# A hybrid gated-DeltaNet and retention layer: a pool of its own for the second merge's matrices, and the transposed v in the projections' PSUM banks with two buffers

## The chip, the cores and the metric

One Trainium2 chip, one of its cores. The metric is the device time of one execution in microseconds (us), the lower the better. TensorE (PE) multiplies matrices into PSUM, VectorE (DVE), ScalarE (ACT) and GpSimd (POOL) work element by element, SyncE (SP) issues most of the DMA transfers; ScalarE and POOL issue some of their own. Each engine takes its instructions strictly in order, so an instruction that waits holds up all that stand behind it on that engine.

## The reference

One layer of a latent transformer over 256 context tokens and 1024 latent tokens, 1024 wide. After an RMS norm with modulation, one input projection feeds two groups of four heads: a gated delta rule (GDN) in both directions and a retention in both directions. Both are normed, gated, projected out and added; a SwiGLU follows, and a last norm. What the change touches is the delta rule, in chunks (the kernel takes 128 tokens as a chunk):

```python
G = jnp.cumsum(gc, axis=-1)
decay = jnp.where(incl, jnp.exp(jnp.where(incl, diff, 0.0)), 0.0)   # diff = G_i - G_j
A = jnp.where(strict, jnp.einsum('nbhid,nbhjd->nbhij', kb, kc) * decay, 0.0)
sol = lax.linalg.triangular_solve(A + jnp.eye(CHUNK), rhs, left_side=True, lower=True, unit_diagonal=True)
qk = jnp.einsum('nbhid,nbhjd->nbhij', qc, kc) * decay
...
v_new = u_c - jnp.einsum('bhck,bhkv->bhcv', w_c, S)
o = jnp.einsum('bhck,bhkv->bhcv', q_c, S) + jnp.einsum('bhij,bhjv->bhiv', qk_c, v_new)
S = gl * S + jnp.einsum('bhck,bhcv->bhkv', k_c, v_new)
```

So for every chunk, head and direction a lower triangular matrix I + A has to be inverted before the scan over the chunks can use it. The norms of k go into the exponent (line 673), which is the "key factors in the exponent" of the kernel's name.

## The kernel before, in words

All matrix products are in float32; a product of full precision is made of three products of split operands (hi and lo parts), which is why the projections come in lines 371, 372, 373 and the convolution's in lines 611, 612, 613. Ten tiles of 128 tokens: 0 and 1 are context, 2 to 9 latent. The program is written in the order of the stages, and a scheduler then mixes the instructions of neighbouring stages on each engine, as far as data, buffers and PSUM banks allow. The order of the work is therefore set by what waits for what, by the order in which a buffer is handed out, and by the scheduler; the rows of it are shown with the change.

The stages in question, in the program's order:

- **Projections** (`token_major`, lines 389 to 399): 24 matrix products per tile and group g of 256 columns, in the PSUM banks "pa" (tile tm, three banks). g 0 and 1 are the retention's v, 2 and 3 its k, 4 and 5 its q, 6 and 7 its gate, 8 and 9 the gate z of the delta rule. They are TensorE's filler wherever another stage waits.
- **Convolution of k, q and v** (`conv_block`, lines 602 to 624): one head is one block of 1280 columns in three chunks in the banks "pc" (tile b), evacuated twice by ScalarE (u and y, lines 614 and 615), four taps on VectorE (line 621), a SiLU (line 624).
- **Preparation of a chunk** (`pre`, lines 700 to 737): products k k' (kk, line 705), transposed q and its norms (qt, lines 710 and 712), k q' (kq, line 715), all in the three banks "pb". For each direction the decays gw come by DMA (line 718), POOL masks them into e (line 722), ScalarE takes exponentials (lines 726 and 735), VectorE multiplies them onto kk and kq (ut and sp, lines 730 and 732), POOL makes the decayed q (line 736), and the results are stored to the scratch tensors un and sd. The pool "gp" holds these tiles, two buffers each.
- **Inversion** (`invert`, lines 743 to 771): the 32x32 diagonal blocks of a batch of chunks are inverted by forward substitution on VectorE: a copy (line 759), 62 operations one after the other (lines 765 and 767), a transposed copy (line 769), and a store to xd. The batches are `BATCH = [[0,1,2,9],[3,8,4,7],[5,6]]`.
- **Merge** (`merge`, lines 791 to 838, with the loads of `blocks`): the whole matrices U (2 MB, line 782) and the inverted blocks, once into U (line 786) and once into t64 (line 787, after a memset by POOL, line 784), then four rounds of small products (lines 806, 813 and 816, 829, 833) in the banks "pb", each with an evacuation by VectorE (xt, lines 809 and 830) or ScalarE (lines 819, 822, 835), and a store to sd (line 837). U and t64 have one buffer in the pool "gm", so the next batch's loads wait until the last one's matrices are stored.
- **The transposed v** (lines 849 to 859): after each head's convolution of v, ten transposes in three groups (vT, in "pb"), copied by ScalarE with a scale into vt (one buffer) and stored by ScalarE's queue.
- **The scan** (`step`, lines 893 to 948): ten steps, both directions side by side; step 0 begins with Tr (line 919) and needs its packed tile pk (line 898). The rest of the projections (g 2 to 5) lies between its first two steps and the others, then the retention.

The program's order is: gate projections, `solve(0)` and `solve(1)` (preparation and inversion of batches 0 and 1), v with its convolution and transposes, preparation of batch 2, `merge(0)`, `invert(2)`, `merge(1)`, `merge(2)`, the z projections, scan. A PSUM ring and a buffer ring hand out their places in this order, whatever the scheduler does.

Of the kernel before, what the change touches and what calls it, by code (L numbers as in the profile page):

```python
# [8 lines left out]
F32 = mybir.dt.float32  # L9
# [8 lines left out]
P = 128  # L18
# [7 lines left out]
H = 4  # L26
# [12 lines left out]
def build(nc, tc, ap, dbg=None, stop=None, marks=None):  # L39
# [3 lines left out]
    def pool(name, bufs=1, side=None, space=None):  # L43
        kw = {}
        if side is not None:
            kw["side"] = side
        if space is not None:
            kw["space"] = space
        if space is not DRAM:
            kw["reuse_waits"] = "tile"  # L50
        es = ExitStack()
        p = es.enter_context(tc.tile_pool(name=name, bufs=bufs, **kw))
        root.push(es)
        p_close[id(p)] = es
        return p
# [3 lines left out]
    def close(p):  # L59
        p_close.pop(id(p)).close()  # L60
# [5 lines left out]
    def checkpoint(name):  # L66
        if dbg is not None:
            marks.append((name, int(nc.cur_bb.bb.instructions[-1].name.split("-")[-1])))
        if stop == name:
            raise Stop()  # L70
# [19 lines left out]
    def bank_a(name):  # L90
        return bank("pa", name)

    def bank_b(name):
        return bank("pb", name)
# [96 lines left out]
    try:  # L191
# [387 lines left out]
        ps = bank_b("G")  # L579
# [14 lines left out]
        ps = bank_b("GT")  # L594
# [5 lines left out]
        CV = pool("cv", side="right")  # L600
# [87 lines left out]
        checkpoint("rg")  # L688
        close(R2)
        close(W2)  # L690
        GP = pool("gp")
        GU = pool("gu")
        GI = pool("gi")

        BATCH = [[0,1,2,9],[3,8,4,7],[5,6]]
        where = {t: (b, c) for b, ch in enumerate(BATCH) for c, t in enumerate(ch)}
# [3 lines left out]
        def pre(t):  # L700
            b, c = where[t]
            kc = load(GP, kd[t], "kc", 2)
            pk = bank_b("kk")
            for h in range(H):
                T.matmul(pk[:, h * P:(h + 1) * P], kc[:, h, :], kc[:, h, :], start=True, stop=True)
            if t >= 2:
                qc = load(GP, qd[t - 2], "qc", 2)
                pn = bank_b("qt")
# [7 lines left out]
            for d in range(2):  # L716
                gw = GP.tile([P, H, P], F32, tag="gw", name="gw", bufs=2)
                SY.dma_start(gw.rearrange("p h i -> p (h i)"),
                             grow_d[c8(t, d), :].rearrange("a b -> (a b)").partition_broadcast(P))
                e = GP.tile([P, H, P], F32, tag="e", name="e", bufs=2)  # L720
                sg = 1 if d == 0 else -1
# [5 lines left out]
                if t >= 2:  # L727
                    sp = GP.tile([P, 2, H, P], F32, tag="sp", name="sp", bufs=2)
                ut = GU.tile([P, H, P], F32, tag="ut", name="ut", bufs=2)
# [13 lines left out]
        def invert(b):  # L743
# [4 lines left out]
            xd = xds[b] = dr.tile([4 * nb, 1024], F32, tag="xd%d" % b, name="xd%d" % b)  # L748
            yr = GI.tile([P, 1024], F32, tag="yr", name="yr", bufs=1)
            for k in range(4):  # L750
                SY.dma_start(yr[k:2 * nb:4].rearrange("r (i j) -> r i j", j=32),
                             un[b][q32[k]].rearrange("i e u j -> (e u) i j")[:, :, q32[k]])
            L = GI.tile([P, 1024], F32, tag="L", name="L", bufs=3)
            X = GI.tile([P, 1024], F32, tag="X", name="X", bufs=2)
# [18 lines left out]
        def blocks(b):  # L773

            nu = len(BATCH[b]) * H
            nb = 4 * nu

            def blk(dram, k):
                return dram.rearrange("(u b) (i j) -> b i u j", b=4, j=32)[k]

            uu = GM.tile([P, 2, len(BATCH[b]), H, P], F32, tag="U", name="U%d" % b, bufs=1)
            SY.dma_start(uu.rearrange("p e c h j -> p e (c h) j"), un[b])
            tt = GM.tile([P, 2, nu, 64], F32, tag="t64", name="t64", bufs=1)
            G.memset(tt, 0.0)
            for k in range(4):
                SY.dma_start(uu[q32[k]].rearrange("p e c h j -> p (e c h) j")[:, :, q32[k]], blk(xds[b][:2 * nb], k))
                SY.dma_start(tt[q32[k]].rearrange("p e u j -> p (e u) j")[:, :, (k % 2) * 32:(k % 2) * 32 + 32],
                             blk(xds[b][2 * nb:], k))
            return uu, [uu[:, 1 - d] for d in range(2)], [tt[:, d] for d in range(2)]
# [59 lines left out]
        for h in range(H):  # L849
            y = newy()  # L850
            conv_block(8 + h, y, False)
            for t0, n in ((0, 2), (2, 4), (6, 4)):
                ps = bank_b("vT")
                for t in range(t0, t0 + n):
                    T.transpose(ps[:, (t - t0) * P:(t - t0 + 1) * P], y[:, t * P:(t + 1) * P], ident)
                vt = CV.tile([P, 4, P], F32, tag="vt", name="vt", bufs=1)
                for t in range(n):
                    S.activation(vt[:, t], ps[:, t * P:(t + 1) * P], AF.Copy, scale=sv3[:, t0 + t, h:h + 1])
                S.dma_start(vd[t0:t0 + n, :, h, :].rearrange("t p j -> p t j"), vt[:, :n])
# [1 line left out]
        checkpoint("v")  # L861
        RP = pool("rp", side="right")
        rope = RP.tile([P, TT, P], F32, tag="rope", name="rope")
        GM = pool("gm")
        for t in BATCH[2]:
            pre(t)
        checkpoint("pre2")
        merge(0)
        SY.dma_start(rope, ap["rope"])
# [7 lines left out]
            token_major(g, LAT, fin_gate, S, W)  # L877
        checkpoint("rgz")
        close(GM)
        close(GI)  # L880
        close(GU)
        close(GP)


        SC = pool("sc", bufs=2, side="right")
# [764 lines left out]
```

## Time and profile before

| | us |
|---|---|
| median of 3 runs | 1491.97 (1490.93 to 1492.1) |
| profiled execution | 1485.42 |
| its span, first to last instruction | 1483.3 |
| mean granted TensorE clock | 0.977 |
| TensorE busy | 1404.5 (95%) |
| first product kk / first U<-un / first merge product | 282.8 / 401.8 / 432.5 |
| last transposed v on TensorE / last vt copy | 395.5 / 411.3 |
| first step of the scan (Tr) behind the last merge | 540.0 |

Times are counted from the start of the span. An engine's busy time is the union of its instructions' spans; in the groups by line the columns are line, engine, operation, result and operands, count, then busy us and mean ns of one, then idle time in front of them and what ended it. "issue" as a releaser means that the profile shows nothing that was waited for. "SPq" rows are transfers as SyncE issues them.

### The profile page before, as it was taken

Reading aid. Unit: us, or ns where it says so; the run is one execution under the profiler, and the core shown is the slowest. Engines: PE = TensorE matmul, PEld = TensorE weight load, DVE = VectorE, ACT = ScalarE, POOL = GpSimd, SP = SyncE. Lnnn points to the kernel's source line nnn. Section 1 sums busy time; section 2 is a strip of 40 time slices with the busy share of each in tenths; the row PEclk is TensorE's granted clock in tenths of the full one; section 3 lists DMA queues with packets and bytes.
Section 4 is the critical chain, followed back from the end, with each engine's and each line's share of the span. In section 5 each row is a group of like instructions: output and inputs, shape, how many; then the busy total and the mean of one; then the engine's idle time right before and its main releaser. Section 6 shows DMA issues by size and latency. Waiting matters only on the chain.

```text
span 1483.3 us, 24109 instructions
## 1 busy us (share of the span) xinstructions
PE 1404.5 (95%) x8919; PEld 1205.9 (81%) x8919; DVE 974.3 (66%) x1856; ACT 616.4 (42%) x1328; POOL 591.8 (40%) x501
## 2 busy tenths in 40 slices
PE   7999999987979899999799899999999999999997
PEld 2898888976978899899588688877888888788886
DVE  6566789279848345788777876656555555657586
ACT  5543564477451121245444533323333332454444
POOL 0120011133114343234135588999555553334321
PEclk9999999998989899999899999999999999999999
DMA  8536686587687645996633265765222242786863
GB/s 321 210 104 205 188 249 198 181 267 224 202 245 204 236 160 209 415 378 221 218 115 114 86 208 214 265 242 178 107 107 106 106 148 79 240 278 199 297 199 114
DMA packets 176565, 298.14 MB, mean 201 GB/s; under 512 B 43496, under 2 KB 93880, under 8 KB 172096
## 3 DMA queue, kind: packets, MB, share of 16 engines
q1 hardware_dynamic: 124896, 253.17, 49.5%
q10 hardware_dynamic: 49072, 35.83, 7.9%
q0 software_dynamic: 2480, 7.60, 1.5%
q8 instruction: 70, 1.15, 0.3%
q14 instruction: 47, 0.39, 0.1%
HBM read 206.60 MB, written 89.96 MB: 200 GB/s over the span
## 4 chain that ended last, share of the span: by engine, by line
PE 39%; POOL 6%; DMA 2%; issue 1%; DVE 1%; ACT 1%; POOLq 0%; ACTq 0%; DVEq 0%
PE ffn L1341 7%; PE ffn L1339 6%; PE ffn L1340 6%; PE fo L1465 4%; PE fo L1467 4%; PE fo L1466 4%; PE op L1198 2%; PE op L1200 2%; PE op L1199 2%; DMA wd<-tw 2%; POOL ws L1312 1%; POOL tw L1393 1%; POOL tw L1392 1%; POOL tw L1395 1%; POOL tw L1394 1%
## 5 line engine op out<-in xcount | busy, mean ns | idle before, releaser
L371 PE MATMUL tm<-whi,hhi 128*128 128x256 f32 (+1 forms) x704 | 201.3, 289 | 4.5 <-ACT xa L384 1.8
L372 PE MATMUL tm<-wlo,hhi 128*128 128x256 f32 (+1 forms) x704 | 201.8, 288 | 2.7 <-DVE wlo L345 2.7
L373 PE MATMUL tm<-whi,hlo 128*128 128x256 f32 (+1 forms) x704 | 199.5, 287 | 0.0
L371 PEld LDWEIGHTS tm<-whi,hhi 128*128 128x128 f32 x704 | 134.2, 192 | 8.7 <-ACT xa L384 2.5
L372 PEld LDWEIGHTS tm<-wlo,hhi 128*128 128x128 f32 x704 | 135.1, 192 | 4.9 <-DVE wlo L345 3.3
L1339 PE MATMUL ffn<-t,whi 128*128 128x512 f32 x352 | 136.9, 390 | 1.4 <-ACT whi L344 1.4
L1341 PE MATMUL ffn<-t,wlo 128*128 128x512 f32 x352 | 137.0, 390 | 0.8 <-DVE wlo L345 0.8
L1340 PE MATMUL ffn<-t,whi 128*128 128x512 f32 x352 | 137.0, 389 | 0.0
L373 PEld LDWEIGHTS tm<-whi,hlo 128*128 128x128 f32 x704 | 134.4, 192 | 0.9 <-DVE hlo L314 0.2
L344 ACT ACTIVATE whi<-wraw 128x512 fp32r<-128x512 f32 (+2 forms) x98 | 75.1, 770 | 136.0 <-PE ffn L1340 81.9
L344 ACT ACTIVATE whi<-ws 128x512 fp32r<-128x512 f32 x88 | 55.6, 632 | 171.6 <-PE ffn L1340 123.9
L345 DVE TENSOR_TENSOR wlo<-ws,whi 128x512 fp32r<-128x512 f32 x88 | 96.0, 1092 | 45.4 <-ACT whi L344 45.2
L1465 PE MATMUL fo<-whi,ahi 128*128 128x512 f32 x308 | 119.3, 389 | 0.9 <-ACT ahi L344 0.9
L1466 PE MATMUL fo<-wlo,ahi 128*128 128x512 f32 x308 | 119.9, 389 | 0.0
L1467 PE MATMUL fo<-whi,alo 128*128 128x512 f32 x308 | 119.0, 390 | 0.0
L345 DVE TENSOR_TENSOR wlo<-wraw,whi 128x512 fp32r<-128x512 f32 (+2 forms) x92 | 98.6, 1073 | 17.7 <-ACT whi L344 17.6
L1339 PE MATMUL ffn<-b,whi 128*128 128x512 f32 x264 | 104.2, 395 | 4.1 <-ACT whi L344 4.1
L1341 PE MATMUL ffn<-b,wlo 128*128 128x512 f32 x264 | 103.9, 393 | 0.7 <-DVE wlo L345 0.7
L1340 PE MATMUL ffn<-b,whi 128*128 128x512 f32 x264 | 103.7, 393 | 0.0
L611 PE MATMUL b<-hhi,whi 128*128 128x512 f32 (+1 forms) x256 | 95.6, 373 | 2.1 <-ACT y L615 1.9
L613 PE MATMUL b<-hhi,wlo 128*128 128x512 f32 (+1 forms) x256 | 95.2, 372 | 0.0
L612 PE MATMUL b<-hlo,whi 128*128 128x512 f32 (+1 forms) x256 | 95.1, 372 | 0.0
(446 smaller groups left out, 3465.6 us busy)
## 6 DMA issues: line engine op xcount, KB each, us to landing
adaw<-ada_w SPq DMA_DIRECT2D x48, 512.0 KB, 4.9
pk<-sd SPq DMA_DIRECT2D x16, 1536.0 KB, 10.9
wraw<-wfi SPq DMA_DIRECT2D x44, 512.0 KB, 3.6
ar<-ad SPq DMA_DIRECT2D x33, 512.0 KB, 4.5
w<-wfo SPq DMA_DIRECT2D x22, 512.0 KB, 5.7
wd<-tw SPq DMA_DIRECT2D x11, 1024.0 KB, 4.8
ad<-act SPq DMA_DIRECT2D x20, 512.0 KB, 3.0
raw<-wd SPq DMA_DIRECT2D x20, 512.0 KB, 5.1
```

The lines of the kernel that those rows point to most:

```text
L344: S.activation(hi, raw, AF.Copy)
L345: e.tensor_tensor(lo, raw, hi.bitcast(F32), ALU.subtract)
L371: T.matmul(o, hhi[:, k, tsl], whi[:, k % 4, :], start=(k == 0), stop=False)
L372: T.matmul(o, hhi[:, k, tsl], wlo[:, k % 4, :], start=False, stop=False)
L373: T.matmul(o, hlo[:, k, tsl], whi[:, k % 4, :], start=False, stop=(k == KT - 1))
L611: T.matmul(o, whi[:, k, :], hh, start=(k == 0), stop=False)
L1339: T.matmul(o, whi[:, k, :], xhi(xn, slice(0, 4), k), start=(first and k == 0), stop=False, **kw)
L1340: T.matmul(o, whi[:, k, :], xlo(xn, slice(0, 4), k), start=False, stop=False, **kw)
L1341: T.matmul(o, wlo[:, k, :], xhi(xn, slice(0, 4), k), start=False, stop=(k == 3), **kw)
L1465: T.matmul(po[g][i], ahi[:, ts], whi, start=(j == 0 and not kw), stop=False, **kw)
L1466: T.matmul(po[g][i], ahi[:, ts], wlo, start=False, stop=False, **kw)
L1467: T.matmul(po[g][i], alo[:, ts], whi, start=False, stop=(j == FH - 1), **kw)
```

## The change

It has four edits.

1. The transposes vT use the banks "pa" of the projections in place of "pb", and vt has two buffers in place of one.
2. The pool "gp" of the preparation is opened behind "gu" and "gi", and is closed behind the preparation of batch 2 instead of behind the z projections.
3. In its place a new pool "g2" is opened, which holds U and t64 of batch 1. Batches 0 and 2 stay in "gm".
4. "gm" moves to the other side of the memory, where the convolution's buffers (u, y, vt) lay.

Nothing of the arithmetic changes.

```diff
--- before.py
+++ after.py
@@ -688,9 +688,9 @@
         checkpoint("rg")
         close(R2)
         close(W2)
-        GP = pool("gp")
         GU = pool("gu")
         GI = pool("gi")
+        GP = pool("gp")
 
         BATCH = [[0,1,2,9],[3,8,4,7],[5,6]]
         where = {t: (b, c) for b, ch in enumerate(BATCH) for c, t in enumerate(ch)}
@@ -778,9 +778,10 @@
             def blk(dram, k):
                 return dram.rearrange("(u b) (i j) -> b i u j", b=4, j=32)[k]
 
-            uu = GM.tile([P, 2, len(BATCH[b]), H, P], F32, tag="U", name="U%d" % b, bufs=1)
+            at = G2 if b == 1 else GM
+            uu = at.tile([P, 2, len(BATCH[b]), H, P], F32, tag="U", name="U%d" % b, bufs=1)
             SY.dma_start(uu.rearrange("p e c h j -> p e (c h) j"), un[b])
-            tt = GM.tile([P, 2, nu, 64], F32, tag="t64", name="t64", bufs=1)
+            tt = at.tile([P, 2, nu, 64], F32, tag="t64", name="t64", bufs=1)
             G.memset(tt, 0.0)
             for k in range(4):
                 SY.dma_start(uu[q32[k]].rearrange("p e c h j -> p (e c h) j")[:, :, q32[k]], blk(xds[b][:2 * nb], k))
@@ -850,10 +851,10 @@
             y = newy()
             conv_block(8 + h, y, False)
             for t0, n in ((0, 2), (2, 4), (6, 4)):
-                ps = bank_b("vT")
+                ps = bank_a("vT")
                 for t in range(t0, t0 + n):
                     T.transpose(ps[:, (t - t0) * P:(t - t0 + 1) * P], y[:, t * P:(t + 1) * P], ident)
-                vt = CV.tile([P, 4, P], F32, tag="vt", name="vt", bufs=1)
+                vt = CV.tile([P, 4, P], F32, tag="vt", name="vt", bufs=2)
                 for t in range(n):
                     S.activation(vt[:, t], ps[:, t * P:(t + 1) * P], AF.Copy, scale=sv3[:, t0 + t, h:h + 1])
                 S.dma_start(vd[t0:t0 + n, :, h, :].rearrange("t p j -> p t j"), vt[:, :n])
@@ -861,9 +862,11 @@
         checkpoint("v")
         RP = pool("rp", side="right")
         rope = RP.tile([P, TT, P], F32, tag="rope", name="rope")
-        GM = pool("gm")
+        GM = pool("gm", side="right")
         for t in BATCH[2]:
             pre(t)
+        close(GP)
+        G2 = pool("g2")
         checkpoint("pre2")
         merge(0)
         SY.dma_start(rope, ap["rope"])
@@ -877,9 +880,9 @@
             token_major(g, LAT, fin_gate, S, W)
         checkpoint("rgz")
         close(GM)
+        close(G2)
         close(GI)
         close(GU)
-        close(GP)
 
 
         SC = pool("sc", bufs=2, side="right")
```

Line numbers behind line 781 grow by one, behind line 864 by three. What the scheduler makes of it, at three places. First TensorE, around the transposes: b is the convolution of v, kk, qt and kq the products of a chunk's preparation, tm a projection (here z). Before, at the first transposes of all:

```order
L371 MATMUL tm<-whi,hhi 128x256
L372 MATMUL tm<-wlo,hhi 128x256
L373 MATMUL tm<-whi,hlo 128x256
L855 MATMUL vT<-ident,y 128x128 x12
L611 MATMUL b_3980<-hhi,whi 128x512
L612 MATMUL b_3980<-hlo,whi 128x512
L613 MATMUL b_3980<-hhi,wlo 128x512
```

And now, at the last ones, with the preparation of batch 2 (both of its tiles) between the last two heads:

```order
L705 MATMUL kk<-kc 128x128 x3
L856 MATMUL vT<-ident,y 128x128 x10
L705 MATMUL kk<-kc 128x128
L710 MATMUL qt<-ident,qc 128x128 x4
L715 MATMUL kq<-qc,kc 128x128 x4
L705 MATMUL kk<-kc 128x128 x4
L710 MATMUL qt<-ident,qc 128x128 x4
L715 MATMUL kq<-qc,kc 128x128 x4
L856 MATMUL vT<-ident,y 128x128 x10
L371 MATMUL tm<-whi,hhi 128x256
L372 MATMUL tm<-wlo,hhi 128x256
L373 MATMUL tm<-whi,hlo 128x256
```

Before, projections stood between the convolution and the transposes and went on all through them (231 projection products between the first kk and the last vT, 75 more up to the last kq). Now there is none in front of the last vT: they begin behind it, 190 in a row up to the first merge product. In the merges stand 323 where 565 stood, and behind the last merge 735 where 287 stood.

Second SyncE, at the loads of the merges' matrices. Numbers behind un, xd and U are the batch; gw and sp belong to the preparation of batch 2. Before:

```order
L733 DMA un2_2894<-ut_4105 128x512
L782 DMA U0_4171<-un0_2892 128x4096
L737 DMA sd_1296<-sp_4086 128x1024
L737 DMA sd_1296<-sp_4104 128x1024
L718 DMA gw_4153<-grow_d_1295 128x512
L869 DMA rope_4049<-rope 128x1280
L787 DMA t64_4173<-xd0_3079 32x32x32 x4
L733 DMA un2_2894<-ut_4146 128x512
L786 DMA U0_4171<-xd0_3079 32x32x32 x4
L737 DMA sd_1296<-sp_4145 128x1024
L771 DMA xd1_3426<-X_3433 64x1024 x2
L771 DMA xd1_3426<-XT_3531 64x1024 x2
```

And now:

```order
L733 DMA un2_2894<-ut_4164 128x512
L737 DMA sd_1296<-sp_4163 128x1024
L783 DMA U1_4550<-un1_2893 128x4096
L771 DMA xd0_3079<-X_3086 64x1024 x2
L771 DMA xd0_3079<-XT_3184 64x1024 x2
L751 DMA yr_4440<-un2_2894 16x32x32 x2
L783 DMA U0_4175<-un0_2892 128x4096
L872 DMA rope_4049<-rope 128x1280
L751 DMA yr_4440<-un2_2894 16x32x32 x2
L788 DMA t64_4177<-xd0_3079 32x32x32 x4
L787 DMA U0_4175<-xd0_3079 32x32x32 x4
L771 DMA xd1_3426<-X_3433 64x1024 x2
```

U1 is now asked for before U0, and the store of inversion 0 (xd0) follows the whole preparation where it had long been made; the loads of batch 0's blocks stand behind it.

Third VectorE, in front of the first evacuation of merge 0 (xt, line 809, now line 810). tmp and X are the steps of an inversion, XT its transposed copy, wlo a split of a projection's weights. Before:

```order
L767 TENSOR_TENSOR X<-X,tmp 128x2x30
L765 TENSOR_TENSOR tmp<-L,X 128x31
L767 TENSOR_TENSOR X<-X,tmp 128x31
L769 COPY XT<-X 128x1024
L345 TENSOR_TENSOR wlo<-wraw,whi 128x4x256
L730 TENSOR_TENSOR ut<-kk,e 128x512
L732 TENSOR_TENSOR sp<-kq,e 128x512
L345 TENSOR_TENSOR wlo<-wraw,whi 128x4x256
L809 TENSOR_SCALAR xt_4248<-m_4183 128x512
```

And now:

```order
L345 TENSOR_TENSOR wlo<-wraw,whi 128x4x256
L767 TENSOR_TENSOR X<-X,tmp 128x8x24
L765 TENSOR_TENSOR tmp<-L,X 128x175
L767 TENSOR_TENSOR X<-X,tmp 128x7x25
L765 TENSOR_TENSOR tmp<-L,X 128x156
L767 TENSOR_TENSOR X<-X,tmp 128x6x26
L345 TENSOR_TENSOR wlo<-wraw,whi 128x4x256
L765 TENSOR_TENSOR tmp<-L,X 128x135
L810 TENSOR_SCALAR xt_4252<-m_4187 128x512
```

Before, inversion 1 was complete (XT) when merge 0 asked for its first evacuation. Now 58 of its 62 steps and two splits stand between the end of inversion 0 and that evacuation, and the last four behind it. Inversion 2 has moved too: its steps now stand between the evacuations of merges 0 and 1, and its transposed copy in front of merge 1's second pair.

## The prediction

> **What bounds the kernel now.** I read the page first, then the busy time by stage from the first product of the delta rule's preparation to the first step of the scan, then who waits for whom there, and last the single groups of ScalarE and VectorE and the queue of SyncE. The page says which engine carries the span:
>
> ```profile
> PE 1404.5 (95%) x8919; PEld 1205.9 (81%) x8919; DVE 974.3 (66%) x1856; ACT 616.4 (42%) x1328; POOL 591.8 (40%) x501
> ```
>
> TensorE is busy for 1404.5 of 1483.3 us, so an edit is worth what it takes from TensorE's idle time and from the time at a reduced clock. The change touches 276 to 541 us. In the next rows the columns are the stretch, its length, then PE, PEld, DVE, ACT and POOL busy, the granted clock, the DMA share and GB/s.
>
> ```profile
> 276.00:293.00 17.00, 17.00 (x107) 15.15 (x107) 5.09 (x6) 10.96 (x28) 3.21 (x4) 1.00 0.61 186
> 293.00:359.00 66.00, 54.91 (x309) 48.53 (x308) 53.38 (x76) 50.56 (x138) 29.32 (x24) 0.89 0.79 255
> 359.00:366.00 7.00, 6.86 (x28) 5.36 (x27) 6.79 (x15) 2.94 (x9) 2.21 (x2) 0.82 1.01 216
> 366.00:432.00 66.00, 54.33 (x430) 52.94 (x429) 48.36 (x104) 35.31 (x91) 8.65 (x8) 0.93 0.77 219
> 432.00:541.00 109.00, 97.94 (x1705) 93.35 (x1704) 55.96 (x149) 21.91 (x36) 39.31 (x73) 0.93 0.65 201
> 541.00:593.00 52.00, 52.00 (x449) 51.87 (x447) 26.30 (x97) 8.72 (x14) 19.71 (x37) 1.00 0.58 210
> 458.00:471.00 13.00, 13.00 (x113) 13.00 (x112) 12.52 (x32) 1.87 (x3) 6.26 (x12) 1.00 1.02 306
> ```
>
> Idle TensorE time in the first five is 0 + 11.1 + 0.1 + 11.7 + 11.1 = 34 us. The missing clock, length times (1 - clock), is at most 7.3 + 1.3 + 4.6 + 7.6 = 21 us. So 55 us is all that this stretch can give. The sixth row says that behind it TensorE has no gap. The last row is pure projection: 113 matmuls in 13.0 us, 0.115 us each, my price for work that only moves. Who is waited for:
>
> ```profile
> PE kk L705 <- ACT vt L858: 6.8, 1, 6.8
> PE vT L855 <- ACT qt L712: 5.9, 1, 5.9
> PE m L816 <- DMA U<-xd: 3.5, 2, 2.1
> PE m L806 <- issue: 3.1, 2, 2.8
> PE kk L705 <- issue: 3.0, 2, 2.4
> PE tm L372 <- DVE wlo L345: 2.7, 2, 2.1
> PE m L816 <- issue: 2.3, 1, 2.3
> PE m L813 <- issue: 1.6, 1, 1.6
> ```
>
> The first two are the shared PSUM banks: products (kk) and transposed v (vT) take turns in the same three, so each waits for ScalarE to empty the other's. The m rows are the merges waiting for their matrices.
>
> **The change part by part: what goes.** The vT rows on the projections' banks end the 6.8 and 5.9 us waits, 12.7 us. Behind the 6.8 us stands ScalarE, itself held by a store:
>
> ```profile
> L858 ACT ACTIVATE vt<-vT,svy 128x128 f32<-128x128 f32 x38 | 11.0, 368 | 24.1 <-DMA sd<-vt 24.0
> SPq L787 <- POOL t L784: 21.7, 2, 14.4
> SPq L786 <- DMA U<-un: 14.4, 2, 9.0
> SPq L782 <- DMA sd<-U: 10.6, 4, 4.2
> ```
>
> Two vt buffers let a copy run while the last store flies, so most of the 24.0 us goes. The own pool lets U1 load during merge 0 instead of behind its stores (10.6 us of SyncE waiting); of the merge waits above, about 7 us belong to merge 1 (2.8, 2.1, 1.6 and a little). Gross: 20 us of idle, and the slow clock behind it.
>
> **What it costs: the filler.** The order shows the price. The projections' banks are handed out in the program's order, so no z projection can start before the last vT: between the first product and the last vT stood 231 projection matmuls, now none; from there to merge 0 stood 165, now 190; inside the merges 565, now 323; behind them 287, now 735. The preparation's pace is therefore no longer hidden. It is set by ScalarE, POOL and the gw loads together:
>
> ```profile
> L726 ACT ACTIVATE e<-e,nG 128x128 f32<-128x128 f32 x49 | 16.0, 391 | 13.4 <-POOL e L722 13.4
> L735 ACT ACTIVATE gw<-gw 128x512 f32<-128x512 f32 x13 | 8.0, 616 | 0.0
> POOL e L722 <- DMA gw<-grow_d: 10.4, 4, 3.4
> 292.98 0.62 ACT L735 ACTIVATE gw<-gw 128x512 f32<-128x512 f32 x1
> 358.67 0.62 ACT L735 ACTIVATE gw<-gw 128x512 f32<-128x512 f32 x1
> ```
>
> From the first gw exponential at 293.0 to the thirteenth at 358.7 are twelve intervals in 65.7 us, 5.5 us each, with ScalarE busy 50.6 us and idle 15.1, 1.26 per interval. In the new order the same twelve hold 18 more vt copies (11.0 / 38 = 0.29 us, 5.2 us), six store issues, one more weight copy and four more evacuations of the convolution: about 11 us, 61.5 busy. The last three intervals hold 16 us and the tail to the last vt copy 7. To the sixteenth that is 77.5 us busy. If the added work fills the idle slots the old pace stays: 15 x 5.5 = 82 us. If the 1.26 us stay on top: 77.5 + 18.9 = 96 us. I take 90, nearer the upper, because the idle is waiting for POOL inside the same loop. The first products now stand ahead of 28 convolution matmuls, so I start 4.5 us earlier, at 288.5: sixteenth at 378.5, last vT at about 386 (378 to 393), where the z projections begin. Stage one on TensorE, 276 to 386, is 110 us. Its work is what lies in the first three rows (78.8 us), less the 36 projections there (4), plus what stood behind them: two tiles' products and 24 transposes.
>
> ```profile
> L705 PE MATMUL kk<-kc 128*128 128x128 f32 x80 | 12.6, 308 | 9.8 <-ACT vt L858 6.8 <-issue 3.0
> L715 PE MATMUL kq<-qc,kc 128*128 128x128 f32 x64 | 10.0, 306 | 0.2 <-ACT qt L712 0.2
> L855 PE MATMUL vT<-ident,y 128*128 128x128 f32 x40 | 7.2, 319 | 6.7 <-ACT qt L712 5.9 <-ACT vt L858 0.8
> ```
>
> Ten tiles have a kk and eight a kq, so two tiles are 2 x (1.26 + 1.25) = 5 us, and the transposes 24 x 0.18 = 4: 84 us in all. Idle: 26 us where before it was 11.
>
> **The merges then follow VectorE.** The inversions stand in front of the merges' evacuations in its order:
>
> ```profile
> L767 DVE TENSOR_TENSOR X<-X,tmp 128x31 f32<-128x31 f32 (+15 forms) x62 | 26.3, 424 | 1.6
> L765 DVE TENSOR_TENSOR tmp<-L,X 128x31 f32<-128x31 f32 (+15 forms) x62 | 25.4, 410 | 2.4 <-ACT L L758 0.8
> L345 DVE TENSOR_TENSOR wlo<-wraw,whi 128x1024 fp32r<-128x1024 f32 x7 | 8.5, 1221 | 2.2 <-ACT whi L344 2.2
> 379.62 1.13 DVE L769 COPY XT<-X 128x1024 f32<-128x1024 f32 x1
> 504.91 4.64 SPq L787 DMA_DIRECT2D t<-xd  x4
> 521.87 1.90 SPq L786 DMA_DIRECT2D U<-xd  x4
> t<-xd SPq DMA_DIRECT2D x4, 64.0 KB, 6.8
> xd<-XT SPq DMA_DIRECT2D x2, 128.0 KB, 2.6
> 521.94 0.45 PE L806 MATMUL m<-t,U 32*32 32x32 f32 x32 [0.31 <-issue]
> 540.03 1.16 PE L919 MATMUL Tr<-pk 128*128 128x128 f32 x8
> ```
>
> One inversion is 51.7 / 2 = 25.9 us. Inversion 0 now ends behind the last product's use: 378.5 + 1.5, 19 short steps (some 5.5 us), transposed copy 1.1: 387. In front of merge 0's first evacuation stand 58 steps and two splits, 25 + 2.4 us, and a copy: 415. TensorE is there at 386 + 190 x 0.115 + 1.3 + 28 x 0.115 = 412, so it waits 3 us (0 to 6). Inversion 1 ends at 418, inversion 2 with three evacuations 28 us later, with some waiting 449. Then the round trip: store 0.9 + 2.6, eight issues 4.6 + 1.9, last landing 5 to 7: merge 2 may begin at 465. Before, merge 2 took 540.0 - 521.9 = 18.1 us with 96 projections; with 84 it takes 16.7: scan step 0 at 482. TensorE's own work (513 x 0.115 = 59, merges about 21) would allow 466, so VectorE's chain ends last. Three new waits of 1 to 5 us cost clock as well:
>
> ```profile
> 430.00:435.00 5.00, 5.00 (x145) 4.45 (x146) 2.58 (x4) 1.86 (x3) 0.90 (x1) 0.68 0.94 302
> 475.00:480.00 5.00, 5.00 (x109) 4.94 (x100) 4.83 (x11) 0.00 (x0) 3.64 (x6) 0.74 1.17 233
> ```
>
> These stretches follow the waits of 2.1 (L372) and 2.8 us (L806), and TensorE, never idle in them, lost 1.6 and 1.3 us. I add 3 us: step 0 at 485, 56 us before the present 541. The Trainium skill, "TensorE: Matmul & The Clock Gate", section "Why this matters for your kernels", lets the clock fall only for gaps over some 3 us; by it the added 3 us would be 0 to 2 and the forecast some 2 us lower. These two rows say that shorter waits cost already, and I go by them.
>
> **The sum.** Of those 56 us, 735 - 287 = 448 projections x 0.115 = 51.5 us are work put off behind the merges, where TensorE was full (sixth row) and stays so. Net gain 4.5 us; I take off 0.5 for the hand-over to the later scan, whose order hardly changes. The profiled execution (1485.42 us, span 1483.3) becomes about 1481.4. The median of the runs, 1491.97, lies 6.6 us above it; 4 us off the median is **1488.0**. A measurement here tells some 0.2% (3 us) from no change.
>
> **The rivals.** *Faster, about 1472.* The vt copies fall into ScalarE's idle 15.1 us, the pace stays 5.5 us, stage one ends 8 us earlier, and the merges run without the three waits (8 us more): 1488 - 16. For it: the 24.0 us of vt waits vanish from the same engine. Against: POOL's waits are in series with the pace.
>
> *Slower, about 1501.* The preparation, stripped of its filler, runs at 6.7 us per interval because the vt stores now share the DMA engines (share 0.79 in the second row) with the gw loads that POOL already awaits: 15 x 0.7 = 10.5 us, and a later inversion chain 2.5 more: 1488 + 13. It decides from the point where the last vT ends later than 390 us; there the gain of 4 us is used up. The Trainium skill, "Perfetto Trace Analysis", section "Optimization Strategy", advises to interleave stages that lean on different engines; by that rule the change goes the wrong way, since it takes 231 projections out of a stage paced by ScalarE. The trace bears it out in part: the first three rows, with 36 of the 231 among them, already leave 11.2 us idle.
>
> *The own pool does nothing, about 1494.* Merge 1 needs inversion 1's blocks anyway, so U1's early load only puts its 2 MB (128 x 4096 x 4 bytes) ahead of U0's in the queue and every merge waits for a round trip, 2 us more each: 1488 + 6.
>
> **How the numbers follow.** Forecast 0.36, its own range 1480 to 1495 (stage one 5 us early or late, waits 0 to 6); faster rival 0.26; slower rival 0.26; idle pool 0.12. Faster by over 0.2% (below 1489): 0.22 of the forecast and the faster rival, 0.48. Within: 0.12 of the forecast and half of the idle pool, 0.18. Slower: the slower rival, 0.06 of the pool and 0.02, 0.34. The two outer rivals spread some 6 us around their values, so 1470 to 1503 leaves out about 2 in 10.
>
> **What would show it.** Right: no wait of kk for vt and of vT for qt; no projection between the first kk and the last vT; that vT near 386; step 0 of the scan near 485; waits of m for VectorE or U<-xd of 1 to 5 us before the first evacuation of merge 0 and at merge 2. Wrong: intervals of the gw exponential near 5.5 or above 6.5 us, a last vT before 380 or after 392, merges without waits, or new gaps behind 541.

## The result, and the profile after

| | before | after |
|---|---|---|
| median (us) | 1492.03 (1490.93 to 1492.36, 4 runs) | 1483.04 (1481.17 to 1485.81, 4 runs) |
| ratio, 95% interval | | 0.9943 [0.9925, 0.996] |
| the same, measured again | | 0.9955 [0.9939, 0.9971] |
| first profiled execution: time, span, clock | 1485.42, 1483.3, 0.977 | 1481.17, 1479.4, 0.983 |
| second profiled execution | 1492.02, 1489.9, 0.978 | 1483.64, 1481.9, 0.982 |

The change is faster by 0.45 to 0.57%, 7 to 9 us. The forecast was 1488.0 (1470 to 1503), 4 us faster. The second executions come from the first two experiments, which are the two kernels once more; what one trace shows only by chance, the other does not show.

The page says where the time came from. The line of engine totals of the changed kernel:

```profile
PE 1400.0 (95%) x8919; PEld 1203.0 (81%) x8919; DVE 969.2 (66%) x1856; ACT 613.4 (41%) x1326; POOL 590.5 (40%) x501
```

TensorE was busy for 1404.5 us before and for 1400.0 now, with the same 8919 products. Its idle time is the rest of the span: 78.8 us before, 79.4 now. In the second pair busy fell from 1403.6 to 1397.0 and idle from 86.3 to 84.9. So the kernel did not lose idle time to speak of. What fell is the time that the same products take, and the granted clock points to why. By stretch (length, PE, PEld, DVE, ACT, POOL busy, clock, DMA share, GB/s), the changed kernel, first execution:

```profile
276.00:580.00 304.00, 273.87 (x2980) 258.93 (x2979) 188.97 (x418) 119.16 (x295) 99.09 (x148) 0.95 0.69 217
580.00:760.00 180.00, 160.10 (x1199) 148.81 (x1198) 133.95 (x466) 78.22 (x208) 52.49 (x49) 0.97 0.76 281
```

and the kernel before, its first execution:

```profile
276.00:580.00 304.00, 270.03 (x2905) 254.32 (x2905) 188.54 (x407) 126.42 (x304) 98.16 (x140) 0.93 0.70 218
580.00:760.00 180.00, 163.07 (x1259) 152.71 (x1258) 136.47 (x472) 78.02 (x208) 51.03 (x52) 0.97 0.75 280
```

From 276 to 580 idle fell from 34.0 to 30.1 us and the missing clock, 304 x (1 - clock), from 21 to 15 us. Behind 580, in the scan and the retention, idle rose from 16.9 to 19.9. The gain in the first stretch is partly given back in the second. Now who is waited for in the changed kernel, the rows that answer to those of before:

```profile
PE vT L856 <- ACT y L624: 9.1, 3, 8.5
PE kk L705 <- issue: 7.5, 2, 6.8
PE m L814 <- issue: 6.1, 2, 3.2
PE tm L371 <- ACT vt L859: 2.9, 1, 2.9
PE qt L710 <- issue: 2.5, 1, 2.5
PE m L807 <- DMA t<-xd: 0.8, 2, 0.5
```

The waits of kk for vt and of vT for qt (12.7 us) are gone as forecast. In their place stand, at the end of the preparation, a wait of vT for the last head's SiLU (y, 8.5 us, until 375.9) and one of kk (6.8 us, until 362.6) for which the profile names nothing. The pace of that stage, the first, second and sixteenth exponential of gw, then the last transposes with the first projections behind them, and the second vt wait of ScalarE:

```profile
286.12 0.62 ACT L735 ACTIVATE gw<-gw 128x512 f32<-128x512 f32 x1
287.81 0.62 ACT L735 ACTIVATE gw<-gw 128x512 f32<-128x512 f32 x1
372.31 0.63 ACT L735 ACTIVATE gw<-gw 128x512 f32<-128x512 f32 x1
...
375.86 2.40 PE L856 MATMUL vT<-ident,y 128*128 128x128 f32 x10 [8.52 <-ACT y L624]
377.91 0.56 PE L371 MATMUL tm<-whi,hhi 128*128 128x256 f32 x1
...
386.77 1.14 ACT L859 ACTIVATE vt<-vT,svy 128x128 f32<-128x128 f32 x4 [7.91 <-DMA sd<-vt]
```

Fifteen intervals take 86.2 us, 5.75 each. The last transposed v is through at 378, and from the first kk on no projection stands in front of it: TensorE has there only the convolution of v, the preparation and the transposes. Then the queue of SyncE, the two loads of U (U1 first, then U0), the first merge's blocks, and on the other engines merge 0's first evacuation, the end of inversion 2, the start of merge 2 and the first step of the scan:

```profile
376.26 0.51 SPq L783 DMA_DIRECT2D U<-un  x1
391.45 0.59 SPq L783 DMA_DIRECT2D U<-un  x1
395.44 10.08 SPq L788 DMA_DIRECT2D t<-xd  x4
405.56 3.41 SPq L787 DMA_DIRECT2D U<-xd  x4
...
412.70 0.68 DVE L810 TENSOR_SCALAR xt<-m 128x512 f32<-128x512 f32 x1
445.15 1.03 DVE L769 COPY XT<-X 64x1024 f32<-64x1024 f32 x1
462.77 0.75 PE L807 MATMUL m<-t,U 32*32 32x32 f32 x64
477.57 0.60 PE L922 MATMUL Tr<-pk 128*128 128x128 f32 x3
```

Step 0 of the scan begins at 477.6, both directions together. Before, the direction that stands behind the last merge began at 540.0 (the other one, in other banks, at 506.6). That is 62.4 us earlier, and the span is 3.9 us shorter: 58.5 us are given back behind it.

### The profile page after: what moved, and what is told of

It is laid out like the page before. It is cut to its first block, busy times and chain, and to the rows that moved or that the text cites. A ratio compares the mean times of both kernels' runs of the same rounds, so it can differ in the third digit from the quotient of the medians.

```text
span 1479.4 us, 24109 instructions
## 1 busy us (share of the span) xinstructions
PE 1400.0 (95%) x8919; PEld 1203.0 (81%) x8919; DVE 969.2 (66%) x1856; ACT 613.4 (41%) x1326; POOL 590.5 (40%) x501
## 4 chain that ended last, share of the span: by engine, by line
PE 55%; POOL 6%; DMA 6%; issue 3%; DVE 2%; ACT 2%; SPq 0%; ACTq 0%; POOLq 0%; DVEq 0%
PE ffn L1344 7%; PE ffn L1342 6%; PE ffn L1343 6%; PE fo L1470 5%; PE fo L1468 5%; PE fo L1469 5%; PE tm L371 3%; PE tm L372 3%; PE tm L373 3%; PE op L1201 2%; PE op L1203 2%; PE op L1202 2%; DMA wd<-tw 1%; POOL ws L1315 1%; PE up L929 1%
## 5 line engine op out<-in xcount | busy, mean ns | idle before, releaser
L344 ACT ACTIVATE whi<-wraw 128x512 fp32r<-128x512 f32 (+2 forms) x98 | 75.2, 771 | 159.7 <-PE ffn L1343 81.9
L345 DVE TENSOR_TENSOR wlo<-wraw,whi 128x512 fp32r<-128x512 f32 (+2 forms) x92 | 103.4, 1125 | 23.4 <-ACT whi L344 23.2
```

What stands on the lines that cost most here:

```text
L344: S.activation(hi, raw, AF.Copy)
L345: e.tensor_tensor(lo, raw, hi.bitcast(F32), ALU.subtract)
```

## The experiments

Two theories went into them. Mine: the projections' banks for vT and the pools pay about half each, against the price of the filler that is gone from the first stage. The rivals: the banks alone, or the own pool alone.

**The changed kernel again** (no edit).

> The changed kernel once more, for the size of the gain, since the first profiled executions lie 4.25 us apart and the medians 9.0 us. If the medians tell it: 1483 us, 9 us under the kernel before. If the profiled pair tells it: about 1488, 4 us under. In either case the last transposed v should leave TensorE within 2 us of 378 us and the first step of the scan begin within 3 us of 477.6 us.

1483.33 us (1481.67 to 1491.49), 0.9955 [0.9939, 0.9971]. The last transposed v began at 376.8 us, step 0 at 477.5. The medians told the size, not the first pair of profiles.

**The kernel before again** (no edit).

> The kernel before once more, against itself. Ratio 1.000 within 0.002 in any theory. If its first profiled execution (1485.42 us, 6.6 us under the median of 1491.97) was a lucky one, this one takes 1489 to 1493 us and shows more idle TensorE time or a lower mean clock than 0.977 somewhere; if the profile itself makes the kernel faster, it is near 1485 again.

1491.92 us against 1491.91, 0.9998 [0.9985, 1.001]; its profiled execution took 1492.02 us. So the first one of 1485.42 was a short one. The same instructions took 3.4 us longer up to step 0 (543.4) and 3.2 more behind it. Clock, idle time and the place of both differ between two executions of one kernel by as much as the change is worth.

**The banks and the second buffer alone**, old pools:

```diff
-                ps = bank_b("vT")
+                ps = bank_a("vT")
-                vt = CV.tile([P, 4, P], F32, tag="vt", name="vt", bufs=1)
+                vt = CV.tile([P, 4, P], F32, tag="vt", name="vt", bufs=2)
```

> The kernel before with the first edit alone: transposes of v in the projections' banks, two vt buffers, old pools. The theory that both parts pay about half each: 1487 to 1488 us, TensorE idle from the first product to the last transposed v about 20 us as in the changed kernel, and merge 1 again waiting for its matrices (about 7 us). The rival that the banks carry all and the own pool does nothing: 1483. The rival that the own pool carries all, because the projections taken out of the preparation cost what the banks give: 1492 or a little above.

1488.45 us, 0.9987 [0.9969, 1.0006].

**The pools alone**: edits 2 to 4 of the change, with `ps = bank_b("vT")` and `bufs=1` left as they were.

> The kernel before with the three pool edits alone: transposes of v stay in the banks of the preparation, one vt buffer. Its order keeps 193 projection products between the first product and the last transposed v (231 before, none in the changed kernel). Both parts half each: 1487 to 1488 us, the waits of kk for vt and of vT for qt still there (12.7 us before), the merges without the waits of merge 1 for its matrices. The banks carry all: 1492. The own pool carries all: 1483.

1490.12 us, 1.0001 [0.9987, 1.0015]. Half each has fallen: the two parts alone give 1.3 permille and nothing, neither clear of zero, together 4.5 to 5.7. With the pools alone vT and kk still share their banks, though their waits for each other have shrunk from 12.7 to 0.7 us without a gain (vT waits 3.0 us for vt). The last transposes come at 393.9 us, and the preparation of batch 2 behind them: its last gw load, the first row here, is issued 11 us later, then U0, the last row, and its last stores only behind U0, up to 424.1 us:

```profile
404.84 0.38 SPq L718 DMA_DIRECT2D gw<-grow_d  x1
405.32 0.74 SPq L737 DMA_DIRECT2D sd<-sp  x1
406.16 0.39 SPq L783 DMA_DIRECT2D U<-un  x1
```

With the banks alone the preparation starts later (first kk at 283.2 us, 275.7 with the pools moved but no own pool, the kernel after next); inversion 0's transposed copy stands at 388.0 instead of 381.2, and the first merge product at 412.2 instead of 399.3. That points to the new place of "gp" in the memory as what the banks need of the pool edits; it was not tried alone.

**The own pool taken back**, everything else changed:

```diff
-            at = G2 if b == 1 else GM
+            at = GM
```

> The changed kernel with the matrices of batch 1 back in the common pool, so that U1 loads behind the stores of merge 0; all other edits stay. Its order puts 577 projections into the merges (323 in the changed kernel). Both parts half each: 1486 to 1488 us, with SyncE again waiting for sd<-U in front of U1 (10.6 us in the kernel before) and merge 1 waiting some 4 to 7 us. The own pool does nothing, since the projections in the merges cover the round trip: 1483. The own pool carries all: 1492.

1485.51 us, 0.9969 [0.9954, 0.9983]. The interval overlaps that of the changed kernel ([0.9939, 0.9971]); the medians lie 2.2 us apart, and the runs don't settle whether the own pool is worth anything. The trace shows both sides of it. In the changed kernel U1's load is issued at 376 us; ScalarE then waits 7.9 us for a vt store (above; 0.9 us at that place without the own pool), U0 follows at 391, and merge 0 begins at 406. Without the own pool:

```profile
384.30 1.82 SPq L783 DMA_DIRECT2D U<-un  x1
...
SPq L783 <- DMA sd<-U: 11.9, 2, 6.0
PE m L817 <- issue: 3.2, 2, 2.5
PE m L814 <- DMA U<-xd: 2.2, 2, 1.7
```

U0 comes 7 us earlier, merge 0 begins at 399.3, SyncE then waits 11.9 us for the stores, and the merges' products (m) wait for 6.0 us, against 6.9 in the changed kernel, with 577 projections in the merges. The last projection is through at 578.4 us, with the own pool at 579.7. Other runs with two vt buffers show the same link. Where the first U load is issued together with the last head's first vt store or up to 3 us ahead of it, ScalarE waits 7.0 to 10.6 us for that store (five executions of four kernels); where the load comes behind all of that head's stores, 0 to 1.9 us (three kernels). In the changed kernel the inversion of batch 1 on VectorE waits 4.6 us for a copy (L, line 758) that stands behind this wait on ScalarE, without the own pool 0.9.

**One buffer, new banks and pools** (`bufs=1` in the changed kernel).

> The changed kernel with one vt buffer; banks and pools stay. If the banks decide: 1483 to 1485 us although ScalarE waits for vt's store longer (11.8 us in the changed kernel, 24.0 before). If the second buffer decides: 1488 to 1490, with the last transposed v 5 us or more later than 377.8.

1493.66 us, 1.0023 [1.0009, 1.0038]: slower than before. Neither side of my expectation, which set banks against buffer, holds. The waits of TensorE and ScalarE, and the stretch behind them:

```profile
PE tm L371 <- ACT vt L859: 11.0, 2, 8.9
PE vT L856 <- ACT y L624: 8.3, 2, 8.0
...
ACT vt L859 <- DMA sd<-vt: 18.3, 5, 9.7
...
364.00:390.00 26.00, 8.88 (x38) 7.82 (x39) 18.97 (x40) 11.07 (x31) 9.46 (x8) 0.50 0.80 281
```

With one buffer ScalarE waits 18.3 us for vt's stores. In the projections' banks these waits stand in front of the projections. The 8.0 us of vT for y are in the changed kernel too (8.5), but the 8.9 us of tm for vt are 2.9 there; between and behind them TensorE runs at half clock for 26 us, with a clock of 0.70 for the same stretch in the changed kernel.

**Two buffers, but the old banks** (`ps = bank_b("vT")` in the changed kernel).

> The changed kernel with the transposes of v back in the banks of the preparation; two vt buffers and the new pools stay. If the banks decide: 1489 to 1491 us, like the kernel with the pools alone (1490.1), with waits of kk and vT for each other of over 5 us again and the last transposed v near 390 us. If the second buffer decides: 1483 to 1485, ScalarE's wait of vt for its store about 12 us as in the changed kernel, the last transposed v near 380.

1490.02 us, 0.9994 [0.9976, 1.0012], the time that stood for the banks, but without the waits that were to come with it: kk waits neither for vT nor for vt (6.6 us, for which the profile names nothing), vT 3.7 us for vt, and the last transposes come at 379.9. What is late is batch 2, whose products stand behind the last transposes in the old ring: the sixteenth exponential of gw begins at 413.5 us (372.3 in the changed kernel, 421.2 with the pools alone), and the transposed copy of inversion 2 at 473.2 (445.1 and 482.8). So the bank seems to pay by this order more than by the waits; the two were not tried apart. With the new pools, bank and buffer are both needed: each without the other gives nothing or costs. This replaces my theory of two halves, as a reading of the traces: the new banks put ScalarE's waits for vt's stores in front of the projections, so they pay only with the second buffer, and the earlier merges only with the pools that are ready for them.

**Four buffers** (`bufs=4`).

> The changed kernel with four vt buffers. If ScalarE's waits for vt's store (3.9 us at 364 and 7.9 us at 379) hold up the last head's SiLU and the first z projections: the waits go, the last transposed v comes 3 to 5 us earlier than 377.8, the wait of 2.9 us of tm for vt goes, and 1480 to 1481.5 us. If the preparation's pace is set by the loads of gw and POOL instead: 1483, the 8.5 us wait of vT for y stays.

1485.99 us, 0.9967 [0.9952, 0.9983], not faster than two; the profiled execution was a long one (1489.38). My theory fell: ScalarE's waits for the vt stores are gone, but TensorE's go elsewhere, and the last transposed v does not come earlier (380.5 us):

```profile
PE kq L715 <- ACT qt L712: 6.4, 1, 6.4
PE tm L371 <- ACT res L532: 5.9, 3, 4.6
PE vT L856 <- ACT y L624: 5.9, 3, 4.0
```

**The last head's transposes in the convolution's banks**, so that projections can start in front of them:

```diff
-                ps = bank_a("vT")
+                ps = bank_a("vT") if h < 3 else bank_c("b2")
```

> The changed kernel with one difference: the last head's transposes of v take the banks of the convolution, the first three heads' those of the projections. Its order has 113 z projections in front of the last transposed v (none in the changed kernel). If the projections' absence in front of the last transposes costs what it seems (one wait of 8.5 us of vT for y, and the clock behind it): that wait goes, 1475 to 1479 us. If VectorE's chain of inversions ends last, the idle time only moves into the merges: 1483, with waits of m for VectorE or U<-xd of 8 us more in sum.

1477.36 us (1475.57 to 1480.05, 6 runs), 0.9917 [0.9896, 0.9938], the time of the filler theory. The wait of vT for y shrinks to 1.0 us, and from 276 to 378 TensorE is busy 89.8 us where it was 81.9. From 378 to 480 it is the other way round:

```profile
276.00:378.00 102.00, 89.78 (x562) 79.12 (x561) 79.03 (x115) 83.04 (x227) 41.99 (x39) 0.97 0.82 260
378.00:480.00 102.00, 83.99 (x1563) 79.57 (x1562) 66.22 (x174) 27.39 (x55) 15.28 (x23) 0.92 0.81 233
...
PE tm L371 <- ACT res L532: 8.9, 3, 6.5
PE tm L371 <- ACT vt L859: 5.2, 1, 5.2
```

The same two stretches of the changed kernel:

```profile
276.00:378.00 102.00, 81.85 (x473) 71.05 (x471) 81.26 (x118) 80.54 (x227) 41.64 (x39) 0.91 0.81 262
378.00:480.00 102.00, 92.02 (x1656) 87.88 (x1655) 64.41 (x166) 28.85 (x58) 11.49 (x17) 0.94 0.85 245
```

So the 8 us of idle time that go in the first stretch come back in the second, as the rival with VectorE's chain had it (one wait there, 3.8 us of m, is for VectorE). Behind 580 us, up to 760, TensorE idles 17.0 us, for 19.9 and 20.8 in the two executions of the changed kernel. The time is that of the filler theory, its mechanism only in part, and where the 6 us come from the runs don't settle.

**Batch 2 prepared ahead of the last head**, whose transposes then go to the preparation's banks:

```diff
         for h in range(H):
+            if h == 3:
+                for t in BATCH[2]:
+                    pre(t)
...
-                ps = bank_a("vT")
+                ps = bank_a("vT") if h < 3 else bank_b("vT")
...
-        for t in BATCH[2]:
-            pre(t)
```

> The changed kernel with the preparation of batch 2 written ahead of the last head of v, and that head's transposes in the banks of the preparation, which nothing follows there but the merges. Its order has 111 z projections in front of the last transposed v. Projections as filler decide: the 8.5 us wait of vT for y goes, 1475 to 1479 us. VectorE's chain decides: about 1483. Sharing of banks decides: above 1486, since vT and kk take turns again at the last head.

1483.6 us, 0.9958 [0.9942, 0.9974], no gain over the changed kernel, though its 111 projections stand in front of the last transposes and the wait for y fell to 2.8 us. The last transposes come later (385.3 us), the first merge product too (422.1, 15.7 us later), and the projections now wait for their results' buffers (1.9, 4.6 and 4.7 us of tm for res). Projections in front are not enough. That merge 0 is put off doesn't explain it: its first product comes later in the faster kernel above too (411.8 us), and in the fastest one below (417.7). From 276 to 480 us TensorE idles as long as in the kernel above, 30.8 us for 30.2; what differs is the clock from 378 on, 0.85 for 0.92:

```profile
378.00:480.00 102.00, 81.86 (x1402) 77.33 (x1401) 65.59 (x172) 30.87 (x58) 13.05 (x19) 0.85 0.76 222
```

**The two pools exchanged** (batches 0 and 2 in the new one):

```diff
-            at = G2 if b == 1 else GM
+            at = GM if b == 1 else G2
```

> The changed kernel with the two pools exchanged: batches 0 and 2 in the new pool, batch 1 in the common one, so that U0 (not U1) is the first matrix loaded, at about 376 us instead of 391. If the load order of the own pool costs time (2 MB of U1 ahead of U0 in the queue, first merge product at 406 us against 399 with U1 in the common pool): the first merge product comes 5 us or more earlier, the wait of 3.2 us at 415 for U<-xd goes, and 1480 to 1481 us. If the projections cover it anyway: 1483. If merge 1 now waits for U1 (loaded from 391 us): 1485.

1488.92 us, 0.9993 [0.998, 1.0007], outside of all three. U0 does load first (377.0 us), and yet the first merge product comes 8.5 us later (414.9) and the last one 7.2 us later (484.6), with as many projections in front of it (510 for 513). Where ScalarE waits for the stores of z, and what TensorE waits for between 580 and 740 us:

```profile
ACT res L532 <- DMA zd<-res: 17.8, 4, 8.6
...
PE ro L1083 <- DMA vg<-rd: 5.7, 1, 5.7
PE rkT L1059 <- DVE qk L1063: 5.5, 1, 5.5
PE Tr L922 <- DVE r L917: 2.8, 4, 1.0
```

The stores of z cost ScalarE 17.8 us (10.4 in the changed kernel). The projections of the later groups end at 599.6 instead of 579.7 us, and the retention waits 11 us in two places where no wait over 2.3 us stood. A pool exchange that reads like one of two loads moves the whole rest of the order; which of these moves costs most was not tried.

**More buffers for the projections' results**, on top of the last head in the convolution's banks:

```diff
-            res = (W2 if early else R1).tile([P, 256], F32, tag="res", name="res", bufs=4 if early else 2)
+            res = (W2 if early else R1).tile([P, 256], F32, tag="res", name="res", bufs=4)
...
-            xt1 = GM.tile([P, 16, 32], F32, tag="xt1", name="xt1", bufs=1)
+            xt1 = GM.tile([P, 16, 32], F32, tag="xt", name="xt1", bufs=1)
-                xt2 = GM.tile([P, 8, 64], F32, tag="xt2", name="xt2", bufs=1)
+                xt2 = GM.tile([P, 8, 64], F32, tag="xt", name="xt2", bufs=1)
```

> The kernel with the last head's transposes in the convolution's banks, and besides four buffers instead of two for a projection's result (res) behind the first two groups; to make room the two evacuation tiles of a merge (xt1, xt2) share one buffer. If the stores of z (zd<-res), held by the loads of U1 and U0, are what stops the projections at 387 and 408 us (6.5 and 1.4 us of tm for res in the profile of the kernel without the extra buffers): those waits go and the half clock behind them, 1469 to 1473 us. If VectorE's inversions end last there: TensorE waits as long in the merges, 1477. If what a stage gains is given back in the scan and the retention, as with the pools exchanged: above 1477, with waits of ro and rkT of over 4 us between 600 and 735.

1473.45 us (1469.81 to 1474.33, 4 runs), 0.9889 [0.9872, 0.9906]: the best version, with an interval that lies wholly below that of the changed kernel, though it overlaps that of the kernel without the extra buffers ([0.9896, 0.9938]). It is just above the range that was expected. One of the two waits, 5.3 us at 389, is still there; the last projection is through at 570.2 us instead of 578.1.

## Why the prediction was right or wrong

**The direction and most of the mechanism** came out: no wait of kk for vt or of vT for qt, no projection in front of the last transposed v, merge 0's first evacuation behind the inversion of batch 1, a step 0 some 60 us earlier, and nearly all of it given back by the projections that follow. A faster kernel had been given a chance of 0.48 only, and some of the prediction's own signs went against it: a last vT before 380 us, no wait of m over 0.5 us before the first evacuation of merge 0 or at the start of merge 2, and 3 us more idle time behind 541.

**Stage one.** Forecast: last vT near 386 (378 to 393), and one before 380 as a sign of being wrong; it was 378. The start was 2.4 us earlier (286.1 for 288.5), fifteen intervals took 86.2 instead of 90, the tail to the first projection 5.6 (372.3 to 377.9) instead of 7. The pace of 5.75 us lies nearer the lower bound (5.5) than the 6.0 that I took: ScalarE's wait for POOL (e, over the whole preparation) fell from 16.3 to 11.9 us, so part of the added copies may have gone into it. Of its 24.0 us of waits for vt's stores, of which "most" was to go, 11.8 stayed. TensorE idled 20.2 us up to 378, for a forecast 26. The slower rival, 6.7 us per interval, did not come; the faster rival's stage one did.

**The merges.** First evacuation 412.7 for 415, transposed copy of inversion 2 done at 446.2 for 449, merge 2 at 462.8 for 465, step 0 at 477.6 for 485. VectorE works on the inversion without a gap up to the first evacuation, so the chain does set that date. The two waits of m (3.2 and 2.9 us, until 418.6 and 445.7) are not the ones forecast: they fall into the middle of a round, behind its evacuation and 9 us or more behind the issue of its blocks, and the profile names nothing for them. The 7.4 us by which step 0 came before 485 are 2.2 at the start of merge 2, 1.9 in merge 2 (14.8 us for 16.7) and the 3 that were added for the clock of TensorE. That term was put on top of a chain that VectorE was said to set, and the chain came without it.

**What is given back** was sized too small: 51.5 + 0.5 us forecast, 58.5 measured (58.0 in the second pair: step 0 from 543.4 to 477.5, span from 1489.9 to 1481.9). The price of a projection was right, 61.0 / 525 = 0.116 us:

```profile
480.00:541.00 61.00, 61.00 (x525) 61.00 (x524) 27.85 (x86) 7.65 (x10) 27.11 (x54) 1.00 0.57 203
```

448 of them are 52 us. The term that was sized wrong is the 0.5 us for the hand-over, with "where TensorE was full (sixth row) and stays so": it was 6.5. TensorE is full up to 580 us, but besides the 448 projections 49 more products of the scan stand between step 0 and the last projection (140 for 91), some 6 us by what the two stretches (102.4 us now, 44.1 before) leave beside the projections. Of these 49, 8 are the other direction's of step 0 (at 506.6 before), and 41 stood behind the last projection before. Yet both kernels take 899 us behind it: from 580 to 760 TensorE idles 3.0 us more than before (3.7 in the second pair: 17.1 to 20.9 us).

**The two errors cancel** in the profiled execution, by luck: 62.4 us gained up to step 0 for a forecast 56 (counted from 541; by its own row, from 540.0, it was 55), 6.5 more given back; 1481.4 was forecast for it and 1481.17 measured. **The size of the median's change was wrong**: 9.0 us for 4. I carried the 6.6 us between the profiled execution of before and its median over to the changed kernel, where the profiled execution lies 1.9 us under the median. The second pair of executions differs by 8.4 us, as the medians do, and there the errors don't cancel: 65.9 us were gained up to step 0, and 58.0 given back for a forecast 52.

**The gross sum counted the wrong thing.** It took 20 us from idle time, "and the slow clock behind it" as an extra. In both pairs the idle time of the whole span moved by 1.4 us or less, the busy time of the same products by 4.5 and 6.6. The forecast let three new waits cost 3 us of clock more and credited nothing for the waits that went. What short waits cost, which the prediction weighed by two rows, has its answer too: behind a wait of qt of 2.5 us (until 328.3) and one of m of 2.9 (until 445.7) the changed kernel shows

```profile
330.00:332.00 2.00, 2.00 (x11) 2.00 (x11) 1.83 (x7) 1.99 (x6) 0.00 (x0) 0.50 0.47 76
446.00:448.00 2.00, 2.00 (x67) 1.94 (x52) 0.18 (x1) 1.34 (x3) 0.00 (x0) 0.50 0.97 385
```

a TensorE without a gap at half clock. The Trainium skill, "TensorE: Matmul & The Clock Gate", section "Why this matters for your kernels", asks that gaps stay under some 3 us; here gaps a little under that were followed by half clock as well. That the gap is the cause was not tried by itself.

**The rival "own pool does nothing"** can't be told from the forecast by the own pool itself, whose worth the runs don't settle; its time, 1494, did not come. U1's load does stand ahead of U0's, and merge 0 is 7 us later than without the own pool. But with U0 loaded first (the pools exchanged) it came later still, so the order of the two loads is not shown to be the cause. The pool edits as a whole are needed. The rival was written as if the own pool were all of them, and so was my credit of 7 us for it.

**The rule on interleaving.** The forecast set the slower rival beside the Trainium skill, "Perfetto Trace Analysis", section "Optimization Strategy", by which stages with different limits are interleaved. The change went against it and was faster; but with 113 projections brought back into the end of the stage it was faster by another 6 us (1483.3 to 1477.4). With 111 brought back another way it was not (1483.6), so the rule alone does not tell which interleaving pays.

## What to carry to other kernels

Two stages that share a ring of PSUM banks wait for each other's evacuations, and the later one in the program's order stands behind the earlier. Moving one to another ring paid here only with a second buffer behind its evacuation and with the pool edits, so such edits are measured together and apart. When work moves to another bank ring, look at who stands behind it in that ring: here the projections stood behind the last transposes, and letting only the last head leave the ring was worth nearly as much again as the change. Forecast a small change from two profiled executions or from the spread of the runs, not from one, and count the granted clock behind each wait as a term of its own, but not on top of a chain that another engine sets.

## What the runs showed of the hardware

Two profiled executions of one and the same kernel differed by 6.6 us (1485.42 and 1492.02), 0.4%, with 8919 products in each and a mean clock within 0.001; TensorE's idle time was 78.8 us in the one and 86.3 in the other. So here one trace of each side could not show the size of a change of half a per cent.

In the kernel with one vt buffer the clock stayed at 0.50 from 364 to 390 us, while TensorE was busy for 8.9 of these 26 us in pieces between waits of 8.0 and 8.9 us.

A 2 MB load in the way of small stores showed in the waits for them: with a U load issued together with a vt store (at most 256 KB) or up to 3 us ahead of it, ScalarE waited 7.0 to 10.6 us for the store in five executions of four kernels; with the load behind it, 0 to 1.9 us in three kernels.
